# Row sums of three score tiles inverted together, the first score behind the last key, and two output tiles closed as a pair

## The chip, the cores and the metric

The kernel runs on one core of a Trainium2 chip. Its metric is the device time of one execution in microseconds (us). Before the change the median of three runs is 1540.67 us (1540.62 to 1540.80).

The engines are named as in the profile: PE (TensorE, matrix products), PEld (loading the weights of those products), DVE (VectorE), ACT (ScalarE), POOL (GpSimd) and SP (SyncE, which issues most transfers). Each has a queue of its own and works through it in order. An instruction that waits holds everything that stands behind it on its engine.

## What is computed

Two layers of a decoder on 512 rows of width 1024. Each layer has a mixer with two groups of heads, cross-attention into 256 memory rows, and an MLP. Each part is normalised before and after and added to the residual.

```python
def reference(x, mem, ...):
    for l in range(DEPTH):                      # DEPTH = 2
        a = hybrid_mixer(rms_norm(x, pre_mix_g[l]), ...)   # 8 dilated + 8 latent heads
        x = x + rms_norm(a, post_mix_g[l])
        c = memory_cross_attention(rms_norm(x, pre_xattn_g[l]), ...)
        x = x + rms_norm(c, post_xattn_g[l])
        hdn = jnp.square(jax.nn.relu(rms_norm(x, pre_mlp_g[l]) @ w_up[l]))
        x = x + rms_norm(hdn @ w_down[l], post_mlp_g[l])
    return x

# inside a head of the mixer (both groups are causal):
s = jnp.einsum('bqhd,bkhd->bhqk', qi, k) * scale          # scores
p = jax.nn.softmax(s, axis=-1)                            # exp, divided by the row sum
o = jnp.einsum('bhqk,bkhd->bqhd', p, v)
```

## The kernel before the change

Rows are worked on in four tiles of 128 (t = 0 to 3), columns in halves of 512 (n = 0, 1). A float32 operand is split into a high and a low part (`xth`/`xtl`, `whi`/`wlo`, `kh`/`kl`), and a product takes three matmuls (L247 to L249). ACT makes the high part (L193 for weights, L203 for transposed rows), DVE the low part (L199, L205).

A layer runs through these stages. First come the value columns `vd` and the queries and keys of the dilated heads. `ev_kd` (L651) takes each finished pair of key heads out of PSUM: ACT writes `kh` (L657), DVE writes `kl` (L663), POOL copies both to the other 64 partitions (L665). Four calls give eight heads. Then `attention()` runs the 16 heads; the latent projections (`ptm`, 128x288 and 128x384 pieces) and the memory products are woven between its steps as fillers. Output projection, cross-attention and the MLP follow.

`scores()` (L473) makes one head: for i = 0 to 3 a tile of 128x(i+1)·128 scores goes to PSUM (`sp`, a pool of two slots, so a tile waits until the one two places ahead of it is read), DVE adds the bias and takes the row extreme (L485, into `P` and `nm`), ACT takes the exponential with the row sum in `rs` (L489), DVE inverts the sum (L490) and POOL multiplies (L491). One head later `transposed_scores()` transposes P on PE (`ptp`), and `weighted_values()` uses it.

While `pinned[0]` is true (from the start of attention until the last latent key tile is evacuated in `ev_ckv`), PE keeps program order through `in_order`, and the exponential of each head's first tile is issued after the last `kh` (`last_key[0]`). Everywhere else a scheduler at build time sets each engine's order from its own estimates.

The MLP's last quarter ends each row tile in `done(t, n)`: a sum of squares on ACT (into `mss`; its scratch `junkp` is a slot of the PSUM pool that also holds the transposes `tp`), a product with the gains `gb` on DVE, and after both halves the post-norm (`pnm` on DVE, the power `pnr` on POOL, two DVE operations per tile). In layer 0 the tile's next norm follows (`n1m`, `n1r`, two products `xn`), then its transposes on PE (`tp`), which open layer 1. In layer 1, tiles 0 and 1 go out through `finish_by_transfer`: POOL adds the residual with an accumulating transfer, SP stores. Tiles arrive in the order 0, 1, 2, 3; later sums of the same quarter (`acc<-wa`, `acc<-we`) stand behind each tile's closing on DVE.

## Time and profile before

| | |
|---|---|
| median of three runs | 1540.67 us |
| the profiled execution: its own time | 1540.44 us |
| its span | 1538.6 us |
| outside the span | 1.84 us |
| granted TensorE clock, mean | 0.995 of full speed |
| busy: PE / PEld / DVE / ACT / POOL | 98% / 82% / 64% / 53% / 16% |

The profiled execution is read as a chain of stages, each with the engine that waits in it. PE starts a 128x512 matmul about every 0.23 us while it is dense (a row shows 0.39 us for one, since they overlap), so its idle time and the stretches at a lower granted clock are what the span has to spare.

### The profile page before, as it was taken

To read this page: it belongs to the slowest core of one execution; us is meant where nothing else is said; L and a number is where in the kernel's file an instruction comes from. 1 tells how busy PE (TensorE), PEld (TensorE's weight loads), DVE (VectorE), ACT (ScalarE), POOL (GpSimd) and SP (SyncE) were. 2 spreads that over 40 slices of the span, in tenths; PEclk is the share of its full clock that TensorE was granted. 3 is DMA by queue.
4 is the path that set the end of the run, shared out by engine and by line. 5 is a ranking of instruction groups with operands and counts; after the bars stand their busy time and mean duration, and the time that the engine had idled before them with its cause. 6 is when DMAs were issued, how large, how long until landed. Compare 5 with 4: busy or idle time off the path is not lost.

```text
span 1538.6 us, 21318 instructions
## 1 busy us (share of the span) xinstructions
PE 1501.9 (98%) x7861; PEld 1261.4 (82%) x7861; DVE 985.1 (64%) x1768; ACT 821.0 (53%) x1578; POOL 253.9 (16%) x441
## 2 busy tenths in 40 slices
PE   9989999999999999999989999999999999999997
PEld 7777788898898888888868877978988988888885
DVE  5556865456459677684964667654654594958667
ACT  5356665355357364645644666654553654546363
POOL 2143621021020000000111455201111100000002
PEclk9999999999999999999999999999999999999999
DMA  6423223513131505153642322243322324060535
GB/s 235 153 81 105 87 78 103 186 56 123 55 110 56 178 28 182 38 175 97 201 121 64 117 93 73 69 151 137 110 83 69 113 72 158 15 191 28 181 85 117
DMA packets 89581, 168.29 MB, mean 109 GB/s; under 512 B 6358, under 2 KB 12164, under 8 KB 89476
## 3 DMA queue, kind: packets, MB, share of 16 engines
q1 hardware_dynamic: 86436, 161.15, 32.6%
q0 software_dynamic: 2752, 5.24, 2.1%
q8 instruction: 62, 1.02, 0.3%
q10 hardware_dynamic: 288, 0.52, 0.1%
q14 instruction: 43, 0.35, 0.1%
HBM read 158.49 MB, written 11.03 MB: 110 GB/s over the span
## 4 chain that ended last, share of the span: by engine, by line
PE 83%; DVE 9%; ACT 3%; issue 3%; POOL 1%; DMA 1%; SPq 0%; DVEq 0%; POOLq 0%; ACTq 0%
PE pfm L248 12%; PE pfm L247 12%; PE pfm L249 12%; PE ptm L247 6%; PE ptm L249 6%; PE ptm L248 6%; PE wa L247 3%; PE wa L248 3%; PE wa L249 3%; PE sp L481 3%; PE op L238 3%; DVE wlo L199 2%; PE ptp L230 2%; PE wc L248 1%; PE wc L247 1%
## 5 line engine op out<-in xcount | busy, mean ns | idle before, releaser
L248 PE MATMUL pfm<-xth,wlo 128*128 128x512 f32 (+1 forms) x896 | 322.4, 360 | 0.6
L247 PE MATMUL pfm<-xtl,whi 128*128 128x512 f32 (+1 forms) x896 | 322.2, 360 | 0.0
L249 PE MATMUL pfm<-xth,whi 128*128 128x512 f32 (+1 forms) x896 | 321.6, 359 | 0.0
L199 DVE SCALAR_TENSOR_TENSOR wlo<-raw,gT,whi 128x512 fp32r<-128x512 f32 (+3 forms) x332 | 229.5, 728 | 125.1 <-ACT whi L193 123.5
L193 ACT ACTIVATE whi<-raw,gT 128x512 fp32r<-128x512 f32 (+2 forms) x324 | 209.6, 697 | 174.0 <-PE pfm L249 87.3
L248 PEld LDWEIGHTS pfm<-xth,wlo 128*128 128x128 f32 x896 | 169.1, 189 | 26.9 <-DVE wlo L199 1.4
L249 PEld LDWEIGHTS pfm<-xth,whi 128*128 128x128 f32 x896 | 169.1, 189 | 25.5 <-issue 0.5
L247 PEld LDWEIGHTS pfm<-xtl,whi 128*128 128x128 f32 x896 | 169.2, 189 | 25.0
L164 ACT ACTIVATE whi<-raw 128x1024 fp32r<-128x1024 f32 x112 | 118.1, 1059 | 130.5 <-PE pfm L249 54.0
L165 DVE TENSOR_TENSOR wlo<-raw,whi 128x1024 fp32r<-128x1024 f32 x112 | 134.7, 1219 | 39.1 <-ACT whi L164 39.1
L1068 POOL DMA_DIRECT2D raw<-in_w_down x8 | 9.8, 1230 | 596.2 <-DVE raw L1071 540.1
L491 POOL TENSOR_SCALAR P<-P,rs 128x128 f32<-128x128 f32 (+3 forms) x128 | 73.3, 578 | 156.2 <-DVE rs L490 66.6
L247 PE MATMUL wa<-wlo,fh 128*128 128x512 f32 x240 | 93.6, 390 | 0.5 <-DVE acc L1153 0.5
L248 PE MATMUL wa<-whi,fl 128*128 128x512 f32 x240 | 93.4, 389 | 0.0
L249 PE MATMUL wa<-whi,fh 128*128 128x512 f32 x240 | 93.4, 389 | 0.0
L489 ACT ACTIVATE P<-P,nm 128x128 f32<-128x128 f32 (+3 forms) x128 | 71.2, 557 | 24.6 <-DVE nm L485 23.9
L185 DVE TENSOR_TENSOR wlo<-raw,whi 128x1024 fp32r<-128x1024 f32 x32 | 39.1, 1222 | 59.4 <-ACT whi L184 58.6
L247 PE MATMUL ptm<-wlo,xth 128*128 128x512 f32 (+2 forms) x192 | 68.4, 357 | 5.2 <-DVE wlo L199 4.4
L184 ACT ACTIVATE whi<-raw 128x1024 fp32r<-128x1024 f32 x32 | 33.9, 1061 | 67.3 <-PE ptm L249 60.2
L1071 DVE TENSOR_TENSOR raw<-raw 128x1024 f32<-128x1024 f32 x56 | 67.8, 1217 | 0.2
L248 PE MATMUL ptm<-whi,xtl 128*128 128x512 f32 (+2 forms) x192 | 66.5, 346 | 0.2 <-DVE xtl L205 0.2
L249 PE MATMUL ptm<-whi,xth 128*128 128x512 f32 (+2 forms) x192 | 66.5, 346 | 0.0
(253 smaller groups left out, 3257.8 us busy)
## 6 DMA issues: line engine op xcount, KB each, us to landing
raw<-in_w_up SPq DMA_DIRECT2D x64, 512.0 KB, 4.6
raw<-in_w_down SPq DMA_DIRECT2D x64, 512.0 KB, 4.2
raw<-in_w_in SPq DMA_DIRECT2D x24, 512.0 KB, 5.6
raw<-in_w_xk SPq DMA_DIRECT2D x16, 512.0 KB, 4.1
raw<-in_w_xv SPq DMA_DIRECT2D x16, 512.0 KB, 3.7
raw<-in_w_mix_out SPq DMA_DIRECT2D x16, 512.0 KB, 4.1
raw<-in_w_xq SPq DMA_DIRECT2D x16, 512.0 KB, 6.2
raw<-in_w_xo SPq DMA_DIRECT2D x16, 512.0 KB, 3.6
```

The lines of the kernel that those rows point to most:

```text
L164: nc.scalar.activation(hi, raw, AF.Copy)
L165: nc.vector.tensor_sub(lo, raw, hi.bitcast(F32))
L193: weight_parts[:] = [nc.scalar.activation(cols(hi, k, False), cols(raw, k, True), AF.Copy, scale=g).ins]
L199: nc.vector.scalar_tensor_tensor(lv, rv, g, hv, op0=OP.mult, op1=OP.subtract)
L238: nc.tensor.matmul(ps, lhsT=lhsT, rhs=rhs, start=start, stop=stop)
L247: in_order(nc.tensor.matmul(ps, lhsT=lh, rhs=rl, start=first, stop=False, skip_group_check=more))
L248: in_order(nc.tensor.matmul(ps, lhsT=ll, rhs=rh, start=False, stop=False, skip_group_check=more))
L249: in_order(nc.tensor.matmul(ps, lhsT=lh, rhs=rh, start=False, stop=last, skip_group_check=more))
L481: in_order(nc.tensor.matmul(sp[:, :L], lhsT=q[:, i * 128:(i + 1) * 128], rhs=k[:, :L], start=n == 0, stop=n == len(parts) - 1))
L489: nc.scalar.activation(Pi, Pi, AF.Exp, bias=nm[:, i:i + 1], scale=-1.0, accum_out=rs[:, i:i + 1])
L491: nc.gpsimd.tensor_scalar(Pi, Pi, rs[:, i:i + 1], 1.0, op0=OP.mult, op1=OP.mult)
L1071: nc.vector.tensor_add(tile_, tile_, more)
```

## The change

Three edits. In `scores()`, the inversion of the row sums and the products on POOL are done for tiles 0 to 2 together once tile 2 has its sum (one 128x3 operation), and for tile 3 alone. In `ev_kd`, the last `kl` is remembered too, and while pinned the DVE operation of a head's first score tile is issued after it; `pinned` is set in layer 0 alone. At the end of the MLP, tiles 0 and 1 are closed together, when both are complete: one `pnm` and one power of 128x2, four DVE operations, and in layer 0 one `n1m`/`n1r` of 128x2 and four products, in layer 1 four accumulating transfers and four stores.

```diff
--- before.py
+++ after.py
@@ -464,7 +464,7 @@
     score_op = [None]
     behind = [None]
     behind_keys = [None]
-    last_key = [None]
+    last_key = [None, None]
     pinned = [False]
 
     def new_scores():
@@ -482,13 +482,19 @@
                                           start=n == 0, stop=n == len(parts) - 1))
                 clk[0] += L * (0.00042 if SPLIT else 0.00167)
             Pi = P[:, OFFS[i]:OFFS[i] + L]
-            score_op[0] = nc.vector.tensor_tensor_reduce(
-                out=Pi, in0=sp[:, :L], in1=tb[:, 512 - L:512], scale=-scale, scalar=3e38, op0=OP.add,
-                op1=OP.min, accum_out=nm[:, i:i + 1]).ins
+            with tc.issue_after(last_key[1]) if pinned[0] and i == 0 else nullcontext():
+                score_op[0] = nc.vector.tensor_tensor_reduce(
+                    out=Pi, in0=sp[:, :L], in1=tb[:, 512 - L:512], scale=-scale, scalar=3e38, op0=OP.add,
+                    op1=OP.min, accum_out=nm[:, i:i + 1]).ins
             with tc.issue_after(last_key[0]) if pinned[0] and i == 0 else nullcontext():
                 nc.scalar.activation(Pi, Pi, AF.Exp, bias=nm[:, i:i + 1], scale=-1.0, accum_out=rs[:, i:i + 1])
-            nc.vector.reciprocal(rs[:, i:i + 1], rs[:, i:i + 1])
-            nc.gpsimd.tensor_scalar(Pi, Pi, rs[:, i:i + 1], 1.0, op0=OP.mult, op1=OP.mult)
+
+            if i >= 2:
+                done = slice(0, 3) if i == 2 else slice(3, 4)
+                nc.vector.reciprocal(rs[:, done], rs[:, done])
+                for q in range(4)[done]:
+                    Pq = P[:, OFFS[q]:OFFS[q] + 128 * (q + 1)]
+                    nc.gpsimd.tensor_scalar(Pq, Pq, rs[:, q:q + 1], 1.0, op0=OP.mult, op1=OP.mult)
             if i in SCORE_STEPS:
                 yield
 
@@ -660,7 +666,7 @@
                 lo = None
                 if SPLIT:
                     lo = unit("kl", dt=WD)
-                    nc.vector.tensor_sub(lo[here, :], ps[here, :], u[here, :].bitcast(F32))
+                    last_key[1] = nc.vector.tensor_sub(lo[here, :], ps[here, :], u[here, :].bitcast(F32)).ins
                     for w in (u, lo):
                         nc.gpsimd.tensor_scalar(w[there, :], w[here, :].bitcast(F32), 1.0, 1.0, op0=OP.mult,
                                                 op1=OP.mult)
@@ -898,7 +904,7 @@
                                                     lambda e, j: v[j][:, c + e * 64:c + (e + 1) * 64]))
                         yield
 
-        pinned[0] = True
+        pinned[0] = l == 0
         weave(attention(), [latent_gen, memory()], lambda: RATIOS[0] if not scored[0] else RATIOS[1])
         OTh = [o[0] for o in outs]
         OTl = [o[1] for o in outs]
@@ -1029,7 +1035,8 @@
 
 
         acc = [[None, None] for _ in range(NT)]
-        ss = [small("mss", 2) for _ in range(NT)]
+        pair_ss = small("mss", 4)
+        ss = [pair_ss[:, 0:2], pair_ss[:, 2:4], small("mss", 2), small("mss", 2)]
         nxh = nxl = None
         gb = None
 
@@ -1071,28 +1078,52 @@
                 nc.vector.tensor_add(tile_, tile_, more)
             return parts_w(tile_)
 
-        def finish_by_transfer(t):
-
-            m = small("pnm", 1)
-            nc.vector.scalar_tensor_tensor(m, ss[t][:, 0:1], EPS, ss[t][:, 1:2], op0=OP.add, op1=OP.add)
+        def close_pair():
+
+
+            v = pair_ss.rearrange("p (t n) -> p t n", t=2)
+            m = small("pnm", 2)
+            nc.vector.scalar_tensor_tensor(m, v[:, :, 0], EPS, v[:, :, 1], op0=OP.add, op1=OP.add)
             r = rpow(m, "pn")
-            for n in range(2):
-                rows, cols = slice(t * 128, (t + 1) * 128), slice(n * 512, (n + 1) * 512)
-                nc.vector.scalar_tensor_tensor(acc[t][n], acc[t][n], r[:, 0:1], gb[n], op0=OP.mult, op1=OP.mult)
-                nc.gpsimd.dma_start(acc[t][n], xmid[rows, cols], accum_op=OP.add)
-                nc.sync.dma_start(out[0, rows, cols], acc[t][n])
+            if l == DEPTH - 1:
+                for t in range(2):
+                    for n in range(2):
+                        rows, cols = slice(t * 128, (t + 1) * 128), slice(n * 512, (n + 1) * 512)
+                        nc.vector.scalar_tensor_tensor(acc[t][n], acc[t][n], r[:, t:t + 1], gb[n], op0=OP.mult,
+                                                       op1=OP.mult)
+                        nc.gpsimd.dma_start(acc[t][n], xmid[rows, cols], accum_op=OP.add)
+                        nc.sync.dma_start(out[0, rows, cols], acc[t][n])
+                return
+            ms = small("n1ms", 4)
+            for t in range(2):
+                for n in range(2):
+                    nc.vector.scalar_tensor_tensor(xs[t][n], acc[t][n], r[:, t:t + 1], xs[t][n], op0=OP.mult,
+                                                   op1=OP.add)
+                    sumsq(xs[t][n], ms[:, 2 * t + n:2 * t + n + 1], scale=1.0 / 32.0)
+                store_x(t, xsave)
+            v = ms.rearrange("p (t n) -> p t n", t=2)
+            m = small("n1m", 2)
+            nc.vector.scalar_tensor_tensor(m, v[:, :, 0], EPS, v[:, :, 1], op0=OP.add, op1=OP.add)
+            r = rpow(m, "n1")
+            hv = (nxh[:, 0:4, :], nxh[:, 4:8, :])
+            lv = (nxl[:, 0:4, :], nxl[:, 4:8, :])
+            for t in range(2):
+                xns = [unit("xn") for _ in range(2)]
+                nc.gpsimd.tensor_scalar(xns[0], xs[t][0], r[:, t:t + 1], 1.0, op0=OP.mult, op1=OP.mult)
+                nc.scalar.activation(xns[1], xs[t][1], AF.Copy, scale=r[:, t:t + 1])
+                put_off(("xt", t), DELAY, lambda t=t, xns=xns: [
+                    transposed(xns[n], n, list(zip(hv, lv)), t) for n in range(2)])
 
         def done(t, n, junk):
 
             sumsq(acc[t][n], ss[t][:, n:n + 1], scale=1.0 / 32.0, junk=junk)
-            by_transfer = l == DEPTH - 1 and t < 2
-            if not by_transfer:
+            if l < DEPTH - 1 or t >= 2:
                 nc.vector.tensor_mul(acc[t][n], acc[t][n], gb[n])
             ready_halves[t] += 1
-            if ready_halves[t] < 2:
+            if ready_halves[t] < 2 or t == 0:
                 return
-            if by_transfer:
-                finish_by_transfer(t)
+            if t == 1:
+                close_pair()
                 return
             add_post_norm(acc[t], ss[t], t, out[0] if l == DEPTH - 1 else None)
             if l < DEPTH - 1:
```

No matmul is added or removed. The build moves rows on the engines. `ISA` is the DVE operation of L485 (the profile calls it CUSTOM_DVE_ANT_0), `xN` means N rows alike in a row.

DVE at the start of layer 0's attention, before:

```order
L663 TENSOR_TENSOR kl<-pfm,kh 64x512 x3
L485 ISA P,nm<-sp,tb 128x128
L485 ISA nm 128x1
L663 TENSOR_TENSOR kl<-pfm,kh 64x512 x3
L199 SCALAR_TENSOR_TENSOR wlo<-raw,gT,whi 128x288
L663 TENSOR_TENSOR kl<-pfm,kh 64x512
L199 SCALAR_TENSOR_TENSOR wlo<-raw,gT,whi 128x288 x3
L663 TENSOR_TENSOR kl<-pfm,kh 64x512
L485 ISA P,nm<-sp,tb 128x256
```

and with the change:

```order
L669 TENSOR_TENSOR kl<-pfm,kh 64x512 x6
L199 SCALAR_TENSOR_TENSOR wlo<-raw,gT,whi 128x288
L669 TENSOR_TENSOR kl<-pfm,kh 64x512
L199 SCALAR_TENSOR_TENSOR wlo<-raw,gT,whi 128x288 x3
L669 TENSOR_TENSOR kl<-pfm,kh 64x512
L486 ISA P,nm<-sp,tb 128x128
L486 ISA nm 128x1
L199 SCALAR_TENSOR_TENSOR wlo<-raw,gT,whi 128x288 x2
L486 ISA P,nm<-sp,tb 128x256
```

The first score operation stood ahead of the last five key parts and of four weight parts; now all eight key parts and four of the weight parts stand ahead of it.

DVE at the end of layer 0's MLP, before:

```order
L1090 TENSOR_TENSOR acc<-acc,gb 128x512
L429 SCALAR_TENSOR_TENSOR pnm<-mss 128x1
L1090 TENSOR_TENSOR acc<-acc,gb 128x512
L432 SCALAR_TENSOR_TENSOR xs<-acc,pnr,xs 128x512 x2
L199 SCALAR_TENSOR_TENSOR wlo<-raw,gT,whi 128x512
L1155 TENSOR_TENSOR acc<-acc,wa 128x512
L385 SCALAR_TENSOR_TENSOR n1m<-n1ms 128x1
L1157 TENSOR_TENSOR acc<-wa,acc 128x512
L429 SCALAR_TENSOR_TENSOR pnm<-mss 128x1
L1155 TENSOR_TENSOR acc<-acc,wa 128x512
L432 SCALAR_TENSOR_TENSOR xs<-acc,pnr,xs 128x512 x2
L1157 TENSOR_TENSOR acc<-wa,acc 128x512
```

and with the change:

```order
L1121 TENSOR_TENSOR acc<-acc,gb 128x512 x2
L1086 SCALAR_TENSOR_TENSOR pnm<-mss 128x2
L199 SCALAR_TENSOR_TENSOR wlo<-raw,gT,whi 128x512
L1100 SCALAR_TENSOR_TENSOR xs<-acc,pnr,xs 128x512 x4
L1186 TENSOR_TENSOR acc<-acc,wa 128x512
L1188 TENSOR_TENSOR acc<-wa,acc 128x512
L1186 TENSOR_TENSOR acc<-acc,wa 128x512
L1106 SCALAR_TENSOR_TENSOR n1m<-n1ms 128x2
L1188 TENSOR_TENSOR acc<-wa,acc 128x512
```

The second pair of `xs` operations came after two of the sums; now all four come first, and the three sums follow in one piece.

PE at the start of layer 1's attention, before:

```order
L481 MATMUL sp<-kh,qs 128x256
L481 MATMUL sp<-kl,qs 128x256
L481 MATMUL sp<-kh,qs 128x384
L481 MATMUL sp<-kl,qs 128x384
L481 MATMUL sp<-kh,qs 128x512
L481 MATMUL sp<-kl,qs 128x512
L247 MATMUL ptm<-wlo,xth 128x288
L248 MATMUL ptm<-whi,xtl 128x288
```

and with the change:

```order
L481 MATMUL sp<-kh,qs 128x256
L481 MATMUL sp<-kl,qs 128x256
L481 MATMUL sp<-kh,qs 128x384
L481 MATMUL sp<-kl,qs 128x384
L247 MATMUL ptm<-wlo,xth 128x288
L248 MATMUL ptm<-whi,xtl 128x288
L481 MATMUL sp<-kh,qs 128x512
L481 MATMUL sp<-kl,qs 128x512
```

Two fillers moved ahead of the 128x512 scores. On DVE the 128x256 score operation moved ahead of the last `kl` there.

## Rows read from the trace of the kernel before

**Rows 1.** By stretch: length, busy of PE, PEld, DVE, ACT, POOL, clock, DMA.

```profile
84.00:95.00 11.00, 7.01 (x33) 5.44 (x31) 8.86 (x25) 8.87 (x21) 8.13 (x13) 0.84 0.27 70
89.00:92.00 3.00, 3.00 (x11) 2.34 (x10) 2.26 (x8) 2.97 (x7) 2.82 (x5) 0.50 0.66 180
745.00:800.00 55.00, 49.44 (x223) 40.43 (x222) 42.39 (x67) 31.25 (x62) 11.56 (x13) 0.94 0.59 177
777.00:781.00 4.00, 4.00 (x14) 3.42 (x14) 3.43 (x7) 2.43 (x5) 1.68 (x2) 0.50 0.41 156
846.00:856.00 10.00, 8.11 (x55) 7.35 (x54) 7.70 (x29) 7.51 (x22) 6.36 (x13) 1.00 0.50 153
```

**Rows 2.** Timeline, layer 0's attention start: start, duration, engine, operation, [idle before <-releaser].

```profile
83.69 0.29 DVE L485 CUSTOM_DVE_ANT_0 P<-sp,tb 128x128 f32<-128x128 f32 x1 [9.68 <-PE sp L481]
...
85.47 0.59 ACT L657 ACTIVATE kh<-pfm 64x512 fp32r<-64x512 f32 x1 [6.79 <-DVE kl L663]
...
86.82 0.52 DVE L199 SCALAR_TENSOR_TENSOR wlo<-raw,gT,whi 128x288 fp32r<-128x288 f32 x1
...
87.39 0.40 PE L247 MATMUL ptm<-wlo,xth 128*128 128x288 f32 x1 [2.90 <-DVE wlo L199]
...
95.30 1.03 POOL L491 TENSOR_SCALAR P<-P,rs 128x512 f32<-128x512 f32 x1
...
96.84 0.29 PE L249 MATMUL ptm<-whi,xth 128*128 128x288 f32 x1
96.97 0.39 PE L481 MATMUL sp<-kh,qs 128*128 128x512 f32 x1
...
97.43 0.82 PE L230 MATMUL ptp<-ident,P 128*128 128x128 f32 x6
```

**Rows 3.** Timeline, end of layer 0's MLP and opening of layer 1.

```profile
762.27 1.41 DVE L432 SCALAR_TENSOR_TENSOR xs<-acc,pnr,xs 128x512 f32<-128x512 f32 x2 [0.46 <-POOL pnr L139]
...
771.41 0.58 ACT L381 ACTIVATE junkp<-acc 128x512 f32<-128x512 f32 x1
...
772.26 1.18 PE L230 MATMUL tp<-ident,xn 128*128 128x128 f32 x8 [2.71 <-POOL xn L417]
...
776.79 1.09 PE L230 MATMUL tp<-ident,xn 128*128 128x128 f32 x4 [2.41 <-DVE xtl L205]
...
785.97 0.99 POOL L139 TENSOR_TENSOR n1r<-n1m,mhalf 128x1 f32<-128x1 f32 x1 [3.70 <-DVE n1m L385]
787.06 0.70 POOL L417 TENSOR_SCALAR xn<-xs,n1r 128x512 f32<-128x512 f32 x1
...
788.86 1.04 PE L230 MATMUL tp<-ident,xn 128*128 128x128 f32 x8
```

**Rows 4.** Timeline, start of layer 1's attention.

```profile
849.35 0.69 DVE L663 TENSOR_TENSOR kl<-pfm,kh 64x512 fp32r<-64x512 f32 x1 [0.94 <-ACT kh L657]
...
850.27 0.42 DVE L485 CUSTOM_DVE_ANT_0 P<-sp,tb 128x256 f32<-128x256 f32 x1
...
850.76 0.50 PE L481 MATMUL sp<-kh,qs 128*128 128x512 f32 x1 [1.32 <-DVE nm L485]
```

**Rows 5.** Timeline, the tail of the kernel.

```profile
1522.32 0.92 POOL L139 TENSOR_TENSOR pnr<-pnm,mhalf 128x1 f32<-128x1 f32 x1
...
1523.27 1.41 DVE L1081 SCALAR_TENSOR_TENSOR acc<-acc,pnr,gb 128x512 f32<-128x512 f32 x2 [2.00 <-POOL pnr L139]
...
1524.60 0.68 DVE L1155 TENSOR_TENSOR acc<-acc,wa 128x512 f32<-128x512 f32 x1
```

**Rows 6.** Two groups: busy us, mean ns | idle; and ns min/median/max, starts, forms.

```profile
L490 DVE RECIPROCAL rs<-rs 128x1 f32<-128x1 f32 x128 | 19.8, 158 | 15.9 <-ACT P L489 14.3
...
L139 POOL TENSOR_TENSOR rkvr<-rkvm,mhalf x2: 1024/1026/1029, 114.6 to 873.8; 128x4 f32<-128x4 f32 x2
```

**Rows 7.** Last product of a head and that head's first transposes, layer 1.

```profile
993.99 0.69 POOL L491 TENSOR_SCALAR P<-P,rs 128x512 f32<-128x512 f32 x1 [1.92 <-DVE rs L490]
...
998.99 0.93 PE L230 MATMUL ptp<-ident,P 128*128 128x128 f32 x7
```

## The prediction

> **What bounds the kernel now.** I read the table by stretch first, then the timeline of the stretches that show idle PE time, and last the groups. PE is the bound: busy in 98% of the span, and the change takes no matmul away. A gain can only come from where PE waits or runs at its lower clock, and from the tail behind its last matmul. The table has three such places that the change touches [rows 1]. From 84 to 95 us PE is busy 7.01 of 11 us, and from 89 to 92 us its granted clock is 0.50 (1.2 instead of 2.4 GHz). From 745 to 800 us it is busy 49.44 of 55, and from 777 to 781 us the clock is 0.50 again. From 846 to 856 us it is busy 8.11 of 10, at full clock. The fourth place is the tail, where DVE closes the output tiles.
>
> At the start of layer 0's attention the score operation of head 0 stands on DVE ahead of five key parts and waits 9.68 us for its matmul, until 83.69 [rows 2]. ACT's next `kh` waits 6.79 us for the `kl` behind it, the weight parts come later still, and PE, which has nothing but weights to wait for at 84.49, waits 2.90 us. It runs at half clock afterwards. At the end of layer 0's MLP PE waits 2.71 us, up to 772.26 [rows 3]. The view names `xn`, but `xn` is ready earlier; 772.26 fits the end of ACT's `junkp` (771.41 + 0.58 and the reading of its sum), which holds the PSUM slot. Then PE waits 2.41 us for `xtl`. At the start of layer 1's attention the 128x512 scores wait 1.32 us for DVE to read the 128x256 tile two slots ahead; DVE had a late `kl` in front of it [rows 4]. In the tail POOL takes tile 1's power at 1522.32, behind the two transfers that it issues for tile 0, DVE waits 2.00 us for it, and `acc<-wa` starts only at 1524.60 [rows 5]. From there DVE and ACT are a chain to the last store.
>
> **Term 1, the row sums: 0.** Per head two inversions of 128x1 go, 64 in all, some 0.158 us each [rows 6]: 10 us of DVE, which is not the bound. No PE wait hangs on an inversion. The products of tiles 0 and 1 are put off until tile 2's sum is there. What counts is the last product against the head's first transpose, and tile 3's still comes last. The three products ahead of it take about 1.5 us and delay it by at most about 1 us, the distance of tile 2's exponential from tile 3's being 0.6 us or more. A head has 5.0 us minus 0.69 us = 4.3 us to spare where I show it [rows 7]. Over all 32 heads only the first and the last of a layer have less: the first has 97.43 − 96.33 = 1.1 us [rows 2]. So this costs nothing, with up to 1 us per layer kept for the upper end.
>
> **Term 2, layer 0's attention start: −1.4.** Now the key parts are done while PE is still on the key products (they need ACT and DVE, both idle there), and the first weight half is ready before 84.49. PE goes on. The second half stands behind `kl` of the last pair: PE ends that product near 83.5, `kh` takes 0.59, `kl` 0.69, the weight part 0.52 [rows 2, 4], so 85.3 to 85.4: a wait of 0.7 instead of 2.9. But the first score operation now stands behind all `kl` and two more weight parts: 85.4 + 2×0.52 + 0.69 + 0.29 + 0.1 = 87.5. PE's third score tile needs that slot and waits about 1.4. The fourth needs the second score operation, behind two more weight parts: 87.5 + 1.04 + 0.42 + 0.1 = 89.0, a wait of 1.1. The second head's third tile waits some 1.3 more for its slot. What replaces 2.9 us is thus four waits, 4.5 us together. With the clock kept, PE's 128x512 scores of the second head would start near 94.7 instead of 96.97 [rows 2]. If the clock falls for 3 us, as in 89 to 92 [rows 1], 128x288 products start every 0.26 instead of 0.13 [rows 2]; part of it hides in the waits, and the point comes near 95.6. PE would be idle for over half of 85 to 89, so I take the second: 1.4. Bounds 0.6 and 2.3.
>
> The trace has a gap of 1.32 us after which the clock stays at 1.00 [rows 1, 4], and one of 2.90 us after which it falls. The Trainium skill (TensorE: Matmul & The Clock Gate, Why this matters for your kernels) warns of long gaps between bursts of matmuls, not of many short ones. By that rule the four short waits leave the clock up, this term is 2.3 and the sum 6.6; no row here shows four such waits in a row.
>
> **Term 3, the hand-over from layer 0 to layer 1: −1.8.** Each step was followed from its start in the trace. Both sums are there at 760.7; gains, `pnm` and a weight part on DVE until 762.8; the power of 128x2 on POOL. No row has that size: 128x1 takes 0.55 to 0.99 and 128x4 takes 1.02 [rows 3, 6], so I take 0.7 to 1.0, and it ends at about the same time as the weight part. Four `xs` at 0.70 [rows 3] end at 765.8. The three sums behind them come 1.5 us later than tile 0 left them before, which nothing on PE needs. ACT has its four sums of squares until 767.7, `n1m` and `n1r` end by 769.1, both of ACT's `xn` by 770.6. `junkp` follows at 770.6 instead of 771.41, so PE's first transposes start near 771.4: 0.8 earlier. The second wait shrinks more: DVE reaches the first `xtl` at 773.2, since the closing of the third tile (two `xs`) now stands behind it instead of ahead. The next transposes start at 774.0 instead of 776.79 [rows 3]. Then DVE becomes the limit (weight parts, `xs`, `xtl`): waits of 0.3 to 0.8 add to some 2 us up to 786. Tile 3's transposes, at 788.86 before, are held by POOL's `xn`, and that stands behind DVE's closing of tile 3, which comes 0.7 earlier: 786.3 + 0.70 = 787.05. Gain 1.8. The bounds: 0.3, if PE stays at half clock as long as before and the waits do not absorb it; 2.6, if POOL's power takes 0.55 rather than 0.99 and PE's own work sets the time (786.2).
>
> **Term 4, layer 1's attention start: −1.2.** The 128x256 score operation now stands ahead of the last `kl`, so it starts at 849.0 instead of 850.27 [rows 4]; two fillers stand ahead of the 128x512 scores and end at 849.7, when the slot is free. The wait of 1.32 goes. The next waits, for the second head's 128x256 and 128x384 slots, come to 0.35 each by DVE's durations, where 0.57 stood before. ACT's first exponential now stands ahead of a `kh`, which delays that key pair by 0.6; its head comes much later. POOL's products of head 0 end near 855.2, when PE arrives at their transposes. Bounds 0.4 (POOL late by 0.8) and 1.6.
>
> **Term 5, the tail: −1.3.** One power of 128x2 from 1519.8, not behind any transfer: 0.7 us. Then four operations at 0.67 us from 1520.6 to 1523.3, and `acc<-wa` starts at 1523.3 instead of 1524.60 [rows 5]. PE's `wa` products end near 1523.4 and its last matmul at 1528.8, before DVE would take it at 1529.0. POOL's four transfers now come in one row and end 0.5 to 1 us earlier. If the power takes 0.92 as in [rows 5], 1.1. Bounds 0.9 and 1.4.
>
> **The rest.** The scheduler also moves some matmuls of the latent queries in both layers; PE has single waits of 0.2 to 0.8 us there and the moved rows lie where it is dense. I take 0, with ±0.8.
>
> **Sum.** 0 + 1.4 + 1.8 + 1.2 + 1.3 = 5.7 us. The profiled execution took 1540.44 us (span 1538.6 plus 1.84 outside); the median is 0.23 above it. 1540.44 − 5.7 + 0.2 = 1535.0. All lower bounds together give a gain of 2.2 − 0.8 = 1.4, all upper ones 8.7.
>
> **The rivals.**
> - *The waits take each other's place.* DVE stays the last to arrive at both starts and at the hand-over, and PE stays at half clock as long as before. Then term 2 is 0.6 or less, term 3 about 0.3, and with 0.4 and 1.2 from the others the gain is 2.5: 1538.2. For it: in both openings DVE has more work ahead of PE's needs than time. Against it: the two largest waits end at instructions that clearly move. Chance 0.19.
> - *The clock stays up in layer 0's start.* 6.6 us, 1534.1; counted with the forecast, since it is inside its range.
> - *The change moves nothing that matters.* If 772.26 is set by something that I don't see and the tail by a transfer (the last stores wait for accumulating transfers), only term 2 is left, and the gain is 1.4: 1539.3. Chance 0.05.
> - *Slower: the batch of products comes late.* POOL's product of 128x512 takes 0.69 in one place and 1.03 in another [rows 2, 7]. If the three batched products and the fourth all stretch and POOL's other work (rotations) gets between, the last one ends later than the transposes need. The point from which it decides is 4.3 us for most heads and 1.1 for the first. Past it each head of 28 pays: 0.3 us past it in each would be 8 us, 1543 after the gains. Nothing in the trace puts POOL, 16% busy, so far behind. Chance 0.06.
>
> **How the numbers follow.** The forecast, 1532.4 to 1537.5, has 0.70. The range reaches from 1532.4 to 1538.9, into the first rival, and leaves out some 0.15. A difference of 0.2% (3.1 us, about what a measurement of this kernel can tell from none) lies at 1537.6. Faster: the forecast and a little of the first rival, 0.73. The same: the rest of it and the third case, 0.20. Slower 0.07.
>
> **What the profile after would show.** Term 2: no wait of 2.9 us near 84.5, the second head's 128x512 scores at 94.7 to 95.6, DVE without a 9.68 us wait. Term 3: first `tp` near 771 less what was gained before (all later times shift by term 2), a second wait under 1 us, and small waits on DVE after it. Term 4: no wait over 0.5 us at the 128x512 scores. Term 5: `acc<-wa` at about 4.2 us behind the pair's `pnm` start, and 1.3 us less from PE's last matmul to the end. Term 1: no new wait at `ptp`. I would be wrong if PE's waits merely moved, if the clock falls for longer than before, or if `ptp` waits for POOL.

## The result and the profile after

The changed kernel takes 1529.4 us (median of four runs, 1528.04 to 1530.0), the kernel before 1540.74 (1540.62 to 1541.41). The ratio is 0.9924, with a 95% interval of 0.9907 to 0.9941: faster by 11.3 us, where 5.7 were forecast. The time lies below the forecast range, 1532.4 to 1538.9. The profiled execution took 1530.0 us with a span of 1528.2.

The first table answers to [rows 1], by stretch in the same columns; the stretches are shifted by what had been gained before them, and the second and fourth are those at half clock.

```profile
84.00:95.00 11.00, 8.57 (x37) 7.36 (x36) 8.39 (x25) 8.79 (x23) 6.61 (x12) 0.69 0.59 163
88.00:94.00 6.00, 5.38 (x19) 4.94 (x20) 4.00 (x16) 4.19 (x13) 2.02 (x4) 0.50 0.66 205
739.00:794.00 55.00, 52.41 (x237) 42.34 (x237) 46.85 (x71) 31.99 (x64) 10.50 (x12) 0.97 0.60 181
771.00:774.00 3.00, 2.75 (x9) 2.39 (x10) 2.92 (x7) 2.63 (x7) 0.15 (x1) 0.50 0.62 234
840.00:850.00 10.00, 10.00 (x69) 9.24 (x67) 8.49 (x29) 8.11 (x23) 5.71 (x13) 1.00 0.56 182
```

PE's idle time fell at all three places, from 3.99 to 2.43 us (11.00 − 8.57), from 5.56 to 2.59 and from 1.89 to nothing. But in layer 0's attention start the clock is now at 0.50 for over 6 us, twice as long as before. The timeline of that start, which answers to [rows 2], shows why the fall from 3.99 to 2.43 us is worth less than it looks.

```profile
85.14 0.40 PE L247 MATMUL ptm<-wlo,xth 128*128 128x288 f32 x1 [0.48 <-DVE wlo L199]
...
87.06 0.44 PE L481 MATMUL sp<-kh,qs 128*128 128x384 f32 x1 [1.01 <-DVE nm L486]
...
88.61 0.80 PE L481 MATMUL sp<-kh,qs 128*128 128x512 f32 x1 [0.94 <-DVE nm L486]
...
96.61 0.93 PE L230 MATMUL ptp<-ident,P 128*128 128x128 f32 x7
```

The wait of 2.90 us has become three, and the products after them run at half clock. The hand-over, to be read beside [rows 3]:

```profile
759.62 1.16 POOL L139 TENSOR_TENSOR pnr<-pnm,mhalf 128x2 f32<-128x2 f32 x1 [10.75 <-DVE pnm L1086]
...
768.33 1.18 PE L230 MATMUL tp<-ident,xn 128*128 128x128 f32 x8 [1.05 <-ACT junkp L381]
...
771.25 1.08 PE L230 MATMUL tp<-ident,xn 128*128 128x128 f32 x4 [0.81 <-POOL pnr L139]
...
781.58 0.55 POOL L139 TENSOR_TENSOR n1r<-n1m,mhalf 128x1 f32<-128x1 f32 x1 [2.92 <-DVE n1m L385]
782.23 0.69 POOL L417 TENSOR_SCALAR xn<-xs,n1r 128x512 f32<-128x512 f32 x1
...
782.98 1.09 PE L230 MATMUL tp<-ident,xn 128*128 128x128 f32 x8 [0.27 <-POOL xn L417]
```

Waits of 2.71 and 2.41 us are now 1.05 and 0.81, and tile 3's power stands at 781.58 instead of 785.97. The half clock is shorter here, not longer: it lasts from 770.6 to 774.1 us, where it lasted from 774.7 to 781.6 before. At the start of layer 1's attention the 128x512 scores follow the two fillers without a wait, where [rows 4] has one of 1.32 us:

```profile
843.46 0.29 PE L247 MATMUL ptm<-wlo,xth 128*128 128x288 f32 x1
843.59 0.29 PE L248 MATMUL ptm<-whi,xtl 128*128 128x288 f32 x1
843.80 0.50 PE L481 MATMUL sp<-kh,qs 128*128 128x512 f32 x1
```

The tail, beside [rows 5]: the power is taken right behind the sums, and `acc<-wa` follows the four operations of the pair.

```profile
1510.46 0.72 POOL L139 TENSOR_TENSOR pnr<-pnm,mhalf 128x2 f32<-128x2 f32 x1 [9.52 <-DVE pnm L1086]
...
1511.22 2.74 DVE L1092 SCALAR_TENSOR_TENSOR acc<-acc,pnr,gb 128x512 f32<-128x512 f32 x4 [0.85 <-POOL pnr L139]
...
1513.87 0.68 DVE L1186 TENSOR_TENSOR acc<-acc,wa 128x512 f32<-128x512 f32 x1
```

**Where the 10.4 us of span went.** Every kernel of this study is compared by the distance between the same instructions of PE in its trace, in us: *start*, from the beginning of the span to the first `sp` matmul; *A*, from there to the first `ptp` (layer 0's attention start); *B*, from there to the 101st `ptp` (which holds the latent query products); *C*, from the last `we` matmul of layer 0 to tile 3's `tp` (the hand-over); *D*, from layer 1's first `sp` to its 11th `ptp`; *E*, 90 `ptp` from there (layer 1's query products); *tail*, from PE's last matmul to the end. Each stretch holds the same number of PE's products in every kernel, idle products aside, so a shorter stretch is time gained.

| kernel | start | A | B | C | D | E | tail |
|---|---|---|---|---|---|---|---|
| before | 83.32 | 14.10 | 109.78 | 19.69 | 17.26 | 102.20 | 9.84 |
| changed | 83.09 | 13.51 | 108.13 | 16.09 | 15.07 | 100.61 | 8.90 |
| row sums alone | 83.56 | 14.10 | 108.10 | 19.01 | 17.02 | 100.59 | 10.05 |
| score order alone | 82.95 | 13.44 | 109.79 | 19.63 | 15.27 | 102.18 | 9.87 |
| pair in layer 0 alone | 83.04 | 13.80 | 109.76 | 16.08 | 17.26 | 102.23 | 10.14 |
| pair in layer 1 alone | 85.85 | 14.82 | 109.78 | 18.91 | 17.27 | 102.17 | 8.77 |
| extra inversions | 84.57 | 12.65 | 108.20 | 16.11 | 15.08 | 100.65 | 8.79 |
| three single inversions | 83.49 | 13.48 | 108.88 | 16.11 | 15.27 | 101.31 | 9.60 |
| all four together | 83.11 | 13.48 | 109.00 | 16.11 | 15.94 | 101.41 | 9.64 |
| filled waits | 83.18 | 11.36 | 108.17 | 16.10 | 15.09 | 100.63 | 9.12 |
| filled waits, again | 83.48 | 11.36 | 108.16 | 16.08 | 15.07 | 100.56 | 9.08 |
| changed, again | 83.63 | 12.59 | 108.10 | 16.09 | 15.07 | 100.58 | 8.97 |
| earlier first score | 83.24 | 12.46 | 108.17 | 16.10 | 15.09 | 100.59 | 9.31 |
| early weights | 85.00 | 10.02 | 108.18 | 16.08 | 15.07 | 100.58 | 9.21 |
| early weights, again | 83.51 | 10.04 | 108.16 | 16.10 | 15.07 | 100.58 | 9.23 |
| early weights and fills | 83.50 | 10.95 | 108.10 | 16.08 | 15.07 | 100.60 | 9.45 |
| early weights and score | 83.50 | 10.07 | 108.17 | 16.09 | 15.08 | 100.60 | 8.81 |
| fills at both | 83.53 | 11.36 | 108.15 | 16.11 | 15.07 | 100.60 | 9.17 |
| two powers | 84.67 | 12.27 | 108.15 | 15.93 | 15.09 | 100.65 | 9.10 |
| layer 1 in PE's old order | 83.89 | 13.31 | 108.14 | 16.98 | 16.65 | 100.59 | 8.79 |

From before to changed: A −0.59, B −1.65, C −3.60, D −2.19, E −1.59, tail −0.94, together −10.56; the start (−0.23) and small shifts elsewhere (+0.37) make it −10.4. The start varies by 2.9 us between executions that have the same instructions there, so medians alone can't settle half a microsecond. A stretch is steadier, but one profile is not exact either: in the four executions that have the old order at the place in question, A is 13.80 to 14.82, C 18.91 to 19.69 and the tail 9.84 to 10.14.

### The profile page after: what moved, and what is told of

Read it like the earlier page. It is cut to its first block, busy times and chain, and to the rows that moved or that the text cites. A ratio compares the mean times of both kernels' runs of the same rounds, so it can differ in the third digit from the quotient of the medians.

```text
span 1528.2 us, 21224 instructions
## 1 busy us (share of the span) xinstructions
PE 1500.1 (98%) x7861; PEld 1260.7 (82%) x7861; DVE 981.5 (64%) x1701; ACT 819.9 (54%) x1578; POOL 251.0 (16%) x438
## 4 chain that ended last, share of the span: by engine, by line
PE 83%; DVE 9%; issue 3%; ACT 2%; POOL 1%; DMA 1%; SPq 0%; DVEq 0%; POOLq 0%; ACTq 0%
PE pfm L248 12%; PE pfm L247 12%; PE pfm L249 12%; PE ptm L247 6%; PE ptm L249 6%; PE ptm L248 6%; PE sp L481 3%; PE wa L247 3%; PE wa L249 3%; PE wa L248 3%; PE op L238 3%; DVE wlo L199 3%; PE ptp L230 2%; PE wc L249 1%; PE wc L247 1%
```

## The experiments

**Each part alone.** The kernel before with one edit of the diff at a time.

```diff
 row sums alone:    the edit in scores(), i >= 2, one inversion of 128x3
 score order alone: issue_after(last_key[1]) and pinned[0] = l == 0
 pair in layer 0 / layer 1 alone: close_pair() for l == 0 / l == 1, else as before
```

> The kernel before with the row sums of tiles 0 to 2 inverted together, and nothing else. Theory: the 3.1 us that the two stretches of the latent queries gave (PE's idle time there fell) come from this edit, so it gains 3.1 us: 1537.6, with 1.5 us of it in each layer between 140 and 200 us of the span and from 902 to 960 us. Rival (the prediction's term 1 with its term for the rest): 0, 1540.7 give or take 0.8, and the gain there belongs to the other edits.

Measured: 1537.68 against 1540.68 us, ratio 0.998 (0.9971 to 0.9989): 3.0 us less. B and E fall by 1.68 and 1.61. The theory holds, and the prediction's 0 doesn't.

> The kernel before with the first score behind the last key in layer 0 and no pinned order in layer 1, and nothing else. Theory: the two attention starts stand by themselves: 0.6 us in layer 0 (the clock stays at half for some 6 us) and 2.1 in layer 1, in all 2.7: 1538.0. Prediction's terms 2 and 4 as written: 2.6, with 1.4 in layer 0 and 1.2 in layer 1. The sum is about the same, the split by stretch tells them apart. Rival: layer 1's gain needs the inversions out of DVE's queue; then 1.2 to 1.8 in all, 1539.2.

Measured: 1537.04, ratio 0.9974 (0.9965 to 0.9984): 3.6 less. A −0.66, D −1.99. The split is the theory's and not the prediction's. The median lies 1.0 below the expected 1538.0, while the two stretches of its trace give 2.65.

> The kernel before with tiles 0 and 1 closed together in layer 0 alone. Theory: the hand-over stands by itself and gives 3.6 us: 1537.1, with the clock at half for one stretch shorter than before and the first two waits at about 1.1 and 0.8 us. Rival: part of it came from layer 1's edits (its order), then the prediction's 1.8: 1538.9.

Measured: 1537.59, ratio 0.9981 (0.9972 to 0.999): 3.1 less. C −3.61, as in the whole change.

> The kernel before with tiles 0 and 1 closed together in layer 1 alone. PE's order is that of before, so nothing changes up to the last quarter of the MLP. Theory: 0.95 us as between the two traces: 1539.8. Prediction's term 5 as written: 1.3, 1539.4. Rival: the tail is ended by a transfer or by SP's stores and only half of it arrives: 0.5, 1540.2.

Measured: 1539.53, ratio 0.9995 (0.9986 to 1.0004): 1.15 less, with no change inside the interval. In its trace the tail is 1.07 us shorter; the profiled execution as a whole is longer because its start took 2.5 us more. The four gains add up to 10.9 of 11.3 us, so within the noise of four such differences the parts don't lean on each other.

**DVE's time or PE's order?** The row sums take operations off DVE, and they also move PE's matmuls, because the scheduler counts differently. The first run gives DVE its work back (two inversions per head of a constant, `mhalf`, into `spare`, which nobody reads) and keeps the order.

```diff
+    spare = const.tile([128, 4], F32, name="spare")
...
                 nc.vector.reciprocal(rs[:, done], rs[:, done])
+                if i == 3:
+                    for q in range(2):
+                        nc.vector.reciprocal(spare[:, q:q + 1], mhalf[:, q:q + 1])
```

> The changed kernel with two more 128x1 inversions per head on DVE (of a constant, result unused), which stand behind the inversion of tile 3; the order of everything else on PE, DVE, ACT and POOL is that of the changed kernel. So DVE has back the 64 operations that the row-sum edit took away, while PE keeps the new order. Order theory (the edit's 3.0 us come from where PE's instructions stand in the two query stretches): no loss, 1529.4, at most 0.4 more. DVE theory (they come from DVE's saved time): up to 3.0 us go back, 1532.4.

Measured: 1531.55 against 1541.42, ratio 0.9937 (0.9923 to 0.995). The groups by shape on DVE show the work that was put back (busy us, mean ns of one | idle before):

```profile
L499 DVE RECIPROCAL spare<-mhalf 128x1 f32<-128x1 f32 x64 | 6.7, 154 | 0.0
L496 DVE RECIPROCAL rs<-rs 128x3 f32<-128x3 f32 x32 | 5.5, 173 | 5.1 <-ACT P L492 5.0
L496 DVE RECIPROCAL rs<-rs 128x1 f32<-128x1 f32 x32 | 5.1, 159 | 7.6 <-ACT P L492 7.6
```

PE's order is that of the changed kernel, product for product. In the heads nothing is lost: B and E stay at 108.20 and 100.65, where the DVE theory wants up to 109.8 and 102.2, so it falls. But the median is 1.7 to 2.2 us above the changed kernel's two (1.2 to 2.0 by the ratios, whose intervals overlap), and the order theory allowed 0.4. One profile can't say where that is lost (its start is 1.5 us longer, its A shorter); it stays open.

The second run keeps POOL's products where the change puts them and takes the three inversions one by one, which brings PE's order back nearly to that of before.

```diff
-            if i >= 2:
-                done = slice(0, 3) if i == 2 else slice(3, 4)
-                nc.vector.reciprocal(rs[:, done], rs[:, done])
+            if i in [2, 3]:
+                done = {2: slice(0, 3), 3: slice(3, 4)}[i]
+                for q in range(4)[done]:
+                    nc.vector.reciprocal(rs[:, q:q + 1], rs[:, q:q + 1])
```

> The changed kernel with three 128x1 inversions in place of the one of 128x3, at the same place; the three products on POOL stay late. PE's order in the two query stretches becomes that of the kernel before (but for a few rows near the second head pair's scores), since the scheduler counts three operations instead of one. Order theory: PE's wait of 0.8 us at the 96x512 scores is back and about 3.0 us are lost: 1532.4. Rival (putting off POOL's products is what gained): nothing lost, 1529.4. DVE theory: 3.0 lost too; the run with extra inversions tells it from the order theory.

Measured: 1532.59, ratio 0.9945 (0.9932 to 0.9957). B and E lose 0.75 and 0.70, not 1.6 each. The wait that the old order has is back; here is PE's timeline in layer 0's query products, in the kernel before and then in this one:

```profile
175.44 0.95 PE L481 MATMUL sp<-ring 96*128 96x512 f32 x3 [0.79 <-DVE nm L485]
```

```profile
174.81 0.96 PE L481 MATMUL sp<-ring 96*128 96x512 f32 x3 [0.72 <-DVE nm L486]
```

In the changed kernel no `sp` waits there: its 96x384 scores come behind the transposes and the `op` product instead of ahead of them. The wait alone doesn't make the 0.75, though. In B, PE is idle for 5.25 us before, 4.23 in the changed kernel and 4.37 in this one, and busy for 104.53, 103.90 and 104.51: the same products took PE 0.6 us less in the changed order, and that is what this run gave back. The other half it kept, and the traces show where. Up to 184 us its products come within 0.2 us of those of before; from 191 us on they are 0.9 earlier. Between lie the only four products of B that stand otherwise than before, and waits of 0.25, 0.23, 0.39 and 0.58 us (184.7 to 190.9 us) are now 0.12 and 0.38. That fits the order theory; no run moves these four alone.

The third run goes further than the change: one inversion for all four tiles.

```diff
-            if i >= 2:
-                done = slice(0, 3) if i == 2 else slice(3, 4)
+            if i in [3]:
+                done = {3: slice(0, 4)}[i]
```

> The changed kernel with the row sums of all four tiles inverted by one 128x4 operation after tile 3, and all four products on POOL behind it: one operation less on DVE per head, the products of tiles 0 to 2 later by about 0.7 us, the last one by about 1.5 to 2. PE's order moves by two dozen rows, most of them in the query stretches and at layer 1's attention start. Theory (a head has 4.3 us to spare, the first head of layer 0 1.1 us): heads lose nothing, the first one up to 1 us, and the moved rows decide within 0.6 either way: 1529.8. Rival (the prediction's slower case: the batch comes late): ptp waits for POOL in many heads, 4 us or more lost, 1533.5.

Measured: 1532.83, ratio 0.9948 (0.9935 to 0.996), 3 us worse than the theory, and near the rival's time by another way. The rival wants `ptp` to wait for POOL in many heads; it does so once, 0.34 us at the start of layer 1. The longest other new wait is for ACT's `PT`:

```profile
187.85 0.55 PE L230 MATMUL ptp<-ident,P 128*128 128x128 f32 x3 [0.69 <-ACT PT L516]
...
850.79 0.66 PE L230 MATMUL ptp<-ident,P 128*128 128x128 f32 x4 [0.34 <-POOL P L497]
```

B, D and E lose 0.9, 0.9 and 0.8, and the tail of this execution 0.7. The mechanism of the prediction's slower rival is there, but in one head out of 32; the rest lies in stretches where PE's rows moved, and was not taken apart. One inversion fewer, and a longer time: on this kernel the row-sum edit is worth what the scheduler makes of it.

**The clock in layer 0's attention start.** Eight executions have the changed kernel's order of PE and of the key and weight parts there. In three the clock is at 0.50 for about 3.4 us and A is 12.3 to 12.7; in five, the one shown above among them, for about 6.8 us, and A is 13.3 to 13.5. The next run puts idle products (of zeros, the result unused) into the two waits of 1.01 and 0.94 us.

```diff
+            if pinned[0] and behind[0] is None and i >= 2:
+                idle = t_ps("idle")[:, 0:256]
+                for _ in range(8):
+                    in_order(nc.tensor.matmul(idle, lhsT=zeros[:, 0:128], rhs=zeros, start=True, stop=True))
             sp = pss.tile([128, 512], F32, tag="s", name="sp")
```

> The changed kernel with eight idle 128x256 products (0.11 us each in the trace, 0.9 us together) ahead of the third and of the fourth score tile of head 0 in layer 0, where PE waits 1.01 and 0.94 us; nothing else moves on PE. It keeps PE busy in those waits. Clock theory (the half clock from 88 to 94 us, with PE busy for 5.5 us of it, is what made term 2 come out at 0.6 instead of 1.4): the granted clock stays at 1.00 or falls later and for one stretch, and 0.8 to 2.2 us are gained: 1527.9. Rival: DVE and ACT set the time there anyway, the second head's tiles wait instead, and at most 0.3 is gained: 1529.2.

Measured: 1528.41, ratio 0.9917 (0.9903 to 0.9931). The same stretch as the first row of the first table, and PE's timeline in it:

```profile
84.00:95.00 11.00, 9.77 (x68) 8.22 (x67) 8.87 (x28) 9.55 (x26) 7.14 (x14) 1.00 0.56 166
```

```profile
85.96 1.05 PE L482 MATMUL idle<-zeros 128*128 128x256 bf16 x8
87.14 0.44 PE L485 MATMUL sp<-kh,qs 128*128 128x384 f32 x1
...
87.59 1.05 PE L482 MATMUL idle<-zeros 128*128 128x256 bf16 x8
88.69 0.50 PE L485 MATMUL sp<-kh,qs 128*128 128x512 f32 x1
...
92.04 0.44 PE L485 MATMUL sp<-kh,qs 128*128 128x384 f32 x1 [0.57 <-DVE nm L490]
```

The scores of the first head start when they did, the clock stays at 1.00, and A is 11.36, 2.15 us less. To see it in the time, both kernels ran again on one chip:

> The changed kernel with sixteen idle products in the two waits of layer 0's first scores, as before, now beside the changed kernel on one chip. Clock theory: the 2.1 us by which its first ptp came earlier in the trace are in the time too, 1.5 to 2.1 us below the changed kernel. Rival (the clock moves PE, but the hand-over, the query stretches or the tail give it back): 0 to 0.7 below.

> The changed kernel itself, its instructions in the same order, on the chip of the next three runs, so that they have it beside them. Every theory: 0.9924 of the kernel before within its interval, 1529.4 give or take 0.8 against 1540.7.

Measured: 1528.59 (1528.04 to 1528.97) against 1529.82 (1529.72 to 1531.38) for the changed kernel. No run of the one reaches the other; the medians differ by 1.2, which is what A lost against the shorter of the two half-clock lengths (11.36 against 12.59). On this chip the half clock is paid for in the time; the run with fills at two places, below, doesn't repeat it.

The next run tries DVE's order instead: the first score operation earlier.

> The changed kernel with the first score operation of head 0 behind the sixth kl of the layer instead of behind the eighth, in layer 0. PE's order is unchanged. The score operation then falls into DVE's idle time of 2.45 us ahead of the seventh kl and would be read at about 83.9 us, so the third tile does not wait (1.01 us less) and the fourth waits for the second tile's operation, about 1 us instead of 0.94; ptm waits 0.3 longer for its weight part. Theory (four waits of DVE replaced one, and each can be taken away by DVE's order): 0.7 to 1.7 us gained, 1528.2. Rival (the waits take each other's place): 0, 1529.4. Slower by 0.5 to 1 if the score operation holds the weight parts as it did in the kernel before.

```diff
-                    last_key[1] = nc.vector.tensor_sub(lo[here, :], ps[here, :], ...).ins
+                    part = nc.vector.tensor_sub(lo[here, :], ps[here, :], ...).ins
+                    if (m, a) == (2, 1):
+                        last_key[1] = part
```

Measured: 1529.75 against 1541.42, ratio 0.9927 (0.9914 to 0.9939). The waits took each other's place: 0.87, 1.13 and 0.98 us for 0.48, 1.01 and 0.94. A is 12.46 with 3.4 us of half clock, as in the changed kernel with as much of it. The rival holds.

Then the weight parts earlier:

```diff
-                if m == 2 and a == 1:
+                if m == 2 and a == 0:
                     behind_keys[0] = last_key[0]
```

> The changed kernel with the weight parts of the latent products allowed behind the fifth kh instead of the sixth. Three weight parts on ACT and DVE then fall into the 2.9 and 2.5 us in which both engines idle ahead of the last key pair (80.4 to 83.3 and 81.5 to 84.0 us), and DVE has about 1.5 us less to do from 84 to 89 us. PE's order is unchanged. Theory (the four waits of the start are DVE's backlog): the ptm wait of 0.48 goes, the two score waits of 1.01 and 0.94 fall to 0.9 together, the clock falls later or for one stretch: 1.0 to 2.5 us gained, 1527.6. Rival (the weight parts wait for their buffers, which PE frees at 79 to 81 us, and hold the seventh kh behind them): 0 or up to 1 lost, 1529.9.

> The changed kernel with the earlier weight parts once more, since one profile doesn't tell whether the clock stays up in it. Theory (with one wait of 1.75 us instead of three within 4 us the clock stays at 1.00 in each execution): 10.0 us again from the first score to the first transposes, against 12.6 to 13.5. Rival (it was luck): the clock at half again for one stretch, 11 to 12 us.

Measured: 1528.9 (1526.38 to 1530.6; ratio 0.992, 0.9908 to 0.9933) and, again, 1527.74 (1527.36 to 1527.94; ratio 0.9914, 0.9901 to 0.9928). A is 10.02 and 10.04, the clock 1.00 in both. The second execution:

```profile
84.00:95.00 11.00, 8.80 (x63) 8.11 (x62) 8.08 (x27) 9.41 (x25) 7.84 (x16) 1.00 0.50 150
```

```profile
87.45 0.44 PE L481 MATMUL sp<-kh,qs 128*128 128x384 f32 x1 [1.74 <-DVE nm L486]
...
91.04 0.44 PE L481 MATMUL sp<-kh,qs 128*128 128x384 f32 x1 [0.46 <-DVE nm L486]
```

The three weight parts went into idle time of ACT and DVE (DVE's ahead of the seventh `kl` fell from 2.45 to 0.92 us in the first execution). What is left is one long wait instead of three. It doesn't shrink to the 0.9 expected, and the sum of the waits hardly changed (2.20 against 2.43 us), yet the clock stays up.

> Both: the earlier weight parts and the sixteen idle products. If the two are worth the same thing (time at half clock), together they give what the fills give alone, about 2.0 to 2.5 us: 1527.2. If the waits and the clock are separate losses, 3.0 to 3.5: 1526.2. If the sixteen products, 1.8 us of PE, now stand where no wait is left, they push the scores back and the sum is below the fills alone: 1528.5.

Measured: 1528.56, ratio 0.9918 (0.9905 to 0.9932); A is 10.95, 0.9 more than without the fills, which now stand in the way. The mechanism of the third case holds; the medians on this chip (1528.9 without the fills) don't tell the two apart.

> Both of DVE's reorderings: the weight parts behind the fifth kh and the first score operation behind the sixth kl. The third score tile then doesn't wait (1.75 us less) and the fourth waits for the second tile's operation, behind the last kl, about 1.4 us. Theory: 0.3 us below the earlier weight parts alone, 9.7 us for the stretch, 1528.6. Rival (the waits take each other's place, as they did with the earlier score alone): 10.0 us, and with the clock at half 11 to 12.

Measured: 1527.6 (1526.9 to 1528.16), ratio 0.9914 (0.9901 to 0.9928); A 10.07. The wait of 1.74 moved to the next tile (1.55) and from 0.46 to 0.72. The rival holds again. The earlier weight parts, a change of one character, have with this kernel the lowest medians here: 1527.7 and 1527.6 us against 1529.4 and 1529.8 for the changed kernel, though not on the same chip; the ratios to the kernel before (0.9914 and 0.9929) lie about as far apart, and their intervals overlap. On the one chip that ran both, 1528.9 stands against 1529.8, and single runs overlap. The shorter A is shown, the shorter time only likely.

**The hand-over.** Both fills: the one above, and `idle` products behind the last `we` matmul. `fill(n)` issues n products of 128x256; its body is left out.

```diff
...
                                 product(g, i, j, last_w[g])
+                        if l == 0 and j == 1:
+                            fill(12)
```

> The changed kernel with idle products in PE's waits at two places: sixteen in layer 0's attention start, as in the run with filled waits, and twelve 128x256 at the hand-over (four ahead of the first four transposes, one between, seven ahead of the first ptm), where PE waits 1.05, 0.43 and 0.81 us. Clock theory: at the hand-over too the half clock follows those waits (from 770.7 to 773.9 us, five 128x512 products at 0.43 instead of 0.23 us), so the clock stays up and 0.5 to 1.2 us are gained there, beside 2.1 in layer 0: about 1527.0 against 1529.4. Rival: DVE, busy 1.94 of 2 us there, sets the hand-over anyway; then the seven products push the ptm back and the hand-over gains 0 or loses 0.3: 1528.0.

Measured: 1529.74 against 1541.03, ratio 0.9923 (0.9911 to 0.9936). The stretch of 764 to 774 us, in the changed kernel, in this one, and in the second run of the changed kernel (clock: the third number from the end):

```profile
764.00:774.00 10.00, 7.70 (x33) 5.80 (x32) 9.92 (x19) 9.45 (x24) 3.05 (x4) 0.83 0.43 145
```

```profile
764.00:774.00 10.00, 8.42 (x49) 6.17 (x49) 9.92 (x17) 9.30 (x21) 4.45 (x6) 1.00 0.32 105
```

```profile
764.00:774.00 10.00, 7.47 (x37) 5.20 (x36) 9.92 (x18) 9.46 (x22) 3.43 (x5) 1.00 0.41 136
```

With the fills the clock is at 1.00, but in the third row it is so without them. Fifteen executions have the new hand-over and no fills there: ten show no half clock, four 3.4 us of it and one 6.8. So the run doesn't show that the fills keep the clock up here. What the fifteen show is what the half clock costs: C is 15.93 to 16.11 in the fourteen with 3.4 us or none, and 16.98 in the one with 6.8 (layer 1 in PE's old order, the same instructions at this place). DVE is busy 9.92 of 10 us in all three rows, and in the changed kernel tile 3's transposes wait for POOL's `xn` at the end. So the rival's mechanism holds as long as the half clock is short. Its time, 1528.0, was missed by 1.7, although A is 11.36 as in the other runs with fills; the profiled execution took 1528.69, and where the slower ones lost it, no trace tells.

The next run splits the pair's power.

```diff
-            r = rpow(m, "pn")
+            r = small("pnr", 2)
+            for t in range(2):
+                nc.gpsimd.tensor_tensor(r[:, t:t + 1], m[:, t:t + 1], mhalf[:, t:t + 1], op=OP.pow)
```

> The changed kernel with the pair's post-norm power taken as two operations of 128x1 on POOL in place of one of 128x2, in both layers; the pair is still closed together and the order is the same on every engine. Theory (what term 3 gained and the prediction undercounted lies in the closing of the pair in one piece, so that DVE no longer closes tile by tile, and in the clock; the single power is worth its own 0.5 to 1.1 us at most, since four xs wait for it): hand-over 0.3 to 0.7 later, tail 0.3 to 0.6 later, in all 1.0: 1530.4. Rival (the batched power itself carries most of the two terms): 2 or more, 1531.5.

Measured: 1530.9, ratio 0.9931 (0.9919 to 0.9944). C is 15.93 and the tail 9.10: the batched power is worth nothing at the first place (two of 128x1 took 1.52 us together, the one of 128x2 1.16) and hardly anything at the second, where 0.2 is within what the tail varies. The median is 1.1 to 1.5 above the changed kernel's and near the expected 1530.4, but in the trace these two places lose 0.04 together; its start is 1.6 longer. What is left for term 3 is the closing in one piece, with `n1r` still one power of 128x2.

**Layer 1's attention start.** PE in program order as before, the first score and exponential free of the last keys.

```diff
-        pinned[0] = l == 0
+        pinned[0] = True
+        l_[0] = l
...
-            with tc.issue_after(last_key[1]) if pinned[0] and i == 0 else nullcontext():
+            with tc.issue_after(last_key[1]) if pinned[0] and l_[0] == 0 and i == 0 else nullcontext():
...
```

The last cut leaves out the same edit on the exponential's line.

> The changed kernel with PE held in program order at layer 1's attention start, as in the kernel before, while DVE's and ACT's first score operations stay free of the last keys. PE's order there is that of before, DVE's and ACT's that of the changed kernel but for a few rows. Prediction's mechanism for term 4 (DVE reads the 128x256 tile before the last kl, so the 128x512 scores do not wait): most of the gain stays, at most 0.9 of 2.1 us lost, 1530.0. Rival (PE's fillers between the score tiles, which the free order allows, are what hides the waits): 1.5 to 2.1 lost, 1531.3.

Measured: 1530.84, ratio 0.9933 (0.9919 to 0.9946). D is 16.65: of 2.19 us only 0.61 are left. PE's timeline there:

```profile
845.13 0.50 PE L482 MATMUL sp<-kh,qs 128*128 128x512 f32 x1 [0.17 <-DVE nm L487]
...
848.99 0.44 PE L482 MATMUL sp<-kh,qs 128*128 128x384 f32 x1 [1.08 <-DVE nm L487]
```

The wait of 1.32 us in [rows 4] is nearly gone, as predicted, but the next one grew from 0.57 to 1.08. In the changed kernel PE is busy for all of 840 to 850 us: the fillers that its free order puts between the score tiles hide the rest. The rival holds.

## Why the prediction was wrong

**The sign and the four places were right, the size was not.** The forecast of 5.7 us missed 5.6 of 11.3. Most of that comes from three terms that were sized too small: in the two traces they gave 3.2, 1.8 and 1.0 us more than forecast, while two others gave 0.8 and 0.4 less. The gain lies above the sum's upper end of 8.7, too.

**"The rest: 0" failed, 3.2 us (B and E).** The prediction saw that the scheduler moves matmuls in the query products and took 0 because "the moved rows lie where it is dense". They lie around a wait of 0.8 us at the 96x512 scores and others of 0.2 to 0.6, and the new order has fewer of them: in layer 0, 1.0 of the 1.65 us is idle time of PE (5.25 to 4.23). The other 0.6 is PE's busy time for the same products, which the prediction took as fixed. Each layer gave 1.6. **Term 1, 0,** was right as it was argued: DVE's 10 us are worth nothing in the heads, and no head waits for POOL's late products. (In two places of each layer the profile now names DVE's inversion as what `ptp` waits for, 0.26 and 0.45 us; at the same places of the kernel before it names ACT's `PT`, 0.22 and 0.39.) The error was to price the edit by the engine on which it saves and not by the order that it causes.

**Term 3, 1.8, came out at 3.6** (2.8 to 3.6 against the four executions with the old hand-over). The early steps held within 0.8 us: PE's last `we` product comes 2.3 us earlier by what was gained before, and shifted by that, the first transposes come at 770.6 (771.4 forecast) and the second at 773.5 (774.0). The step that failed is "DVE becomes the limit (...): waits of 0.3 to 0.8 add to some 2 us", with tile 3 "0.7 earlier". Behind the second transposes there is one wait of 0.27. Tile 3's power comes 2.1 us earlier by the same shift (783.9 against 785.97 in [rows 3]), and its transposes at 785.3, not 787.05. Nor had `xn` held those transposes before: by [rows 3] it ended at 787.06 + 0.70 = 787.76, and PE came to them at 788.86 without a wait, out of a row of products that it had started at half clock. So what PE gained ahead of them arrived. Up to 0.9 us of it is the clock, as the C of 16.98 shows. The upper bound of 2.6 had named PE's own work as the limit, but at 786.2; its other condition, a short power, proved worth nothing: the power took 1.16.

**Term 4, 1.2, came out at 2.2.** The wait of 1.32 went for the reason given, and the run with PE's old order keeps 0.6 of the 2.2. But "two fillers stand ahead of the 128x512 scores" was all that the prediction took from PE's new order, and for the second head it forecast waits of 0.35 each. There are none: these two and the fillers between the second head's tiles are together worth 1.6 us, the larger part.

**Term 2, 1.4, came out at 0.6** between the two profiles. The waits were overestimated (0.48, 1.01, 0.94 and none, for 0.7, 1.4, 1.1 and 1.3), and the clock underestimated: "falls for 3 us, as in 89 to 92". It fell for 6.8, and "if the clock falls for longer than before" was one of the prediction's own signs of being wrong. Both lengths occur with the same instructions, and with the shorter one the term is 1.5 to 1.8. The old order varies as well (A 13.80 to 14.82); between the means of its four executions and of the eight the term is 1.1. So the step that failed took one trace's half clock for a constant. The rule that was weighed, by which short waits leave the clock up, did not hold here in any of the eight executions: it was at 0.50 in each. The Trainium skill (TensorE: Matmul & The Clock Gate, Part 1: The HAM clock gate) says of the start of a kernel that the number of matmuls at the low clock varies from run to run. The eight traces show the same in the middle of one: 3.4 us at half clock in three, 6.8 in five.

**Term 5, 1.3, came out at 0.94** in the two profiles, inside its bounds. The power took the forecast 0.72, and `acc<-wa` came at 1513.87, by the 9.47 us gained before it 1523.34: the forecast value. The rest is behind it, and there the tail of other executions with the pair closed together varies between 8.8 and 9.6.

**The range.** Its lower end leaves out the up to 1 us per layer that term 1 had kept back; that has no bearing here, since the result lies beyond the other end.

**The rivals.** *The waits take each other's place* was true as a mechanism in layer 0's start, twice more in the experiments, but not at the hand-over. *Slower by a late batch* needs one inversion for all four tiles before POOL is seen at all, and then in one head. *The change moves nothing that matters* fell with the hand-over: the first `tp` still waits, 1.05 us, for the `junkp` that the prediction had named, and comes earlier with it.

## What to carry to other kernels

An edit that changes operation counts under a scheduler is priced by the order that it leaves, on the bound engine first: list every moved row next to a wait, and don't take "dense" for free. Look at a stretch in more than one profile before putting a number on it: with the very same kernel, A was 13.51 us in one execution and 12.59 in another. Work on the helper engines' backlog just ahead of the place where the bound engine starts to wait; a reordering inside the backlog only moves the wait. At a place whose end is set by another engine, neither a short half clock nor one operation less counts; closing several tiles in one piece can.
